# A key and value buffer of its own for the prompt's middle group, counts halved with immediates, and norm corrections with per-partition scalars

## The chip, the cores and the metric

The kernel runs on one core of a Trainium2 chip. The core's engines take their instructions in order, each from its own queue: PE (TensorE, matmuls and transposes), DVE (VectorE), ACT (ScalarE), POOL (GpSimd) and SP (SyncE, which here only issues DMAs). The metric is the time of one execution in device microseconds; several executions are made, and their median counts.

## The reference, cut to what matters

One step of a decoder layer, on a prompt of 1024 tokens and on 32 sample tokens (8 sequences of 4) with a paged cache of 8192 positions each. The layer's input is normalised, projected by one wide matrix, and goes to two groups of heads: sparse attention over the 256 best keys of each query, which an indexer chooses, and retention. What the change touches, in the reference's own lines:

```python
def _rmsnorm(x, g):
    xf = x.astype(jnp.float32)
    y = xf * lax.rsqrt(jnp.mean(xf * xf, axis=-1, keepdims=True) + EPS) * g.astype(jnp.float32)
...
    s = jnp.einsum('bqhd,bsd->bqhs', qi.astype(jnp.float32), ki.astype(jnp.float32)) * (D_IDX ** -0.5)
    score = jnp.einsum('bqh,bqhs->bqs', wi.astype(jnp.float32), jax.nn.relu(s))
    score = jnp.where(valid, score, -jnp.inf)
    top_val, top_idx = lax.top_k(score, topk)
```

The keys and values of the prompt (ka and va, 128 columns each) are also outputs.

## The kernel before

The program is written with a tile framework: the text gives a first order of the work, a scheduler turns it into one order for each engine, and pools of buffers decide which tile must wait for which transfer. A tile with the same tag in a pool takes the slots in turn; with bufs=2 the third tile waits until the first one's readers, DMAs among them, are done. The order of each engine is fixed before the program runs.

All matmuls of the projections are made from a high and a low part of x (xh, xl) and of the weights (whi, wlo), three matmuls for one product (proj_b, L257 to L259). ACT makes whi (L179), POOL makes wlo (L181). Tokens are taken in three groups, GRP: 0 to 383, 384 to 767, and 768 to 1055, the last one with the 32 sample tokens at its end.

The stages, in order of time:

- Norms of x, in nine blocks (norm_x): ACT sums squares, `rstd_of` (L233) makes 1/sqrt(v), DVE scales the block (L532), PE transposes it (L223), and ACT and DVE split it into xh and xl (L228, L229). `rstd_of` takes y, the reciprocal of a square root, and makes one correction step y·(1.5 − 0.5·v·y²) in L241 to L244. finish_y calls it nine times more near the end, ahead of the gate.
- The indexer (index_scores, L498 to L504): for each of eight blocks of queries and eight heads, PE makes the products si, ACT the relu r, DVE adds to score, and POOL puts the causal limit on the last 128 columns (affine_select, L504).
- Between these matmuls "units" of the other projections are run: four pairs of query heads (use_qa), keys and values (use_ka and use_va, weights wraw_kava), and gates (use_ga, weights wraw_ga). A staging tile with the tag qst, two buffers in the pool qsp, is shared by all of them: qst in use_qa, kst in use_ka, kvs in use_kv, sga in use_ga. Each of them ends in a DMA out of the tile.
- use_kv (L402), for each group: ACT copies the product into kvs (L406), PE transposes it into kvt (L410), DVE copies that into the second half of kvs (L412), and SP sends it out (L414). For the last group, DVE also copies the sample tokens' part (L416).
- The bisection (bisect_prompt): the 256th best score of each query is found bit by bit, in 15 steps for six blocks of queries. `count` (L651 to L665) counts the scores over a threshold cand: four blocks on DVE (L661, comparison with a sum), two on ACT as sums of signs (js, L657). ACT's sums are turned into counts by L665: cnt times −0.5 plus half the length. Then L680 and L682 choose the next cand. The first count of a bit's value, at threshold 0, runs all six blocks on DVE.
- At the same time the paged index keys of the samples are scored: POOL gathers 128 rows of 2048 (kx, L799), PE transposes them (ptx, L809), ACT copies them (kT, L810), PE multiplies (pox, L813), ACT makes a relu (rl, L816), and PE sums over heads (py, L772 and L775).
- Then retention, the samples' attention, the prompt's attention, the output projection, the norms of finish_y, and the gate.

The pool sx (L748) holds kx, kT, rl, ys, xe and the small tiles of the sample indexer. It is opened ahead of the loop over the pages and closed after it with qsp.

Of the kernel before, what the change touches and what calls it, by code (L numbers as in the profile page):

```python
# [10 lines left out]
F32 = mybir.dt.float32  # L11
# [5 lines left out]
ALU = mybir.AluOpType  # L17
# [103 lines left out]
def tile_step(ctx: ExitStack, tc: tile.TileContext, I, O):  # L121
    nc = tc.nc

    def pool(name, bufs=1, **kw):
        return tc.tile_pool(name=name, bufs=bufs, reuse_waits="tile", **kw)
# [18 lines left out]
    def bank(name, tag="b"):  # L144
        if tag in kept.get("tags", ()):
            return kept["pool"].tile([128, 512], F32, tag="s", bufs=1, name=name)
        return psum["pool"].tile([128, 512], F32, tag=tag, bufs=psum["bufs"][tag], name=name)
# [6 lines left out]
    def C(name, rows=128):  # L154
        o, w = _CW[name]
        return cst[:rows, o:o + w]
# [76 lines left out]
    def rstd_of(ss, rows, scale, name, sp):  # L233

        v = sp.tile(list(ss.shape), F32, tag="rs_v", bufs=2, name=f"rv_{name}")
        nc.vector.tensor_scalar(v[:rows], ss[:rows], scale, EPS, op0=ALU.mult, op1=ALU.add)
        y = sp.tile(list(ss.shape), F32, tag="rs_y", bufs=2, name=f"ry_{name}")
        z = sp.tile(list(ss.shape), F32, tag="rs_z", bufs=2, name=f"rz_{name}")
        nc.scalar.activation(y[:rows], v[:rows], AF.Sqrt)
        nc.vector.reciprocal(y[:rows], y[:rows])  # L240
        nc.vector.tensor_tensor(z[:rows], y[:rows], y[:rows], op=ALU.mult)  # L241
        nc.vector.tensor_tensor(z[:rows], z[:rows], v[:rows], op=ALU.mult)
        nc.vector.tensor_scalar(z[:rows], z[:rows], -0.5, 1.5, op0=ALU.mult, op1=ALU.add)
        nc.vector.tensor_tensor(y[:rows], y[:rows], z[:rows], op=ALU.mult)  # L244
        return y


# [133 lines left out]
    qsp = sxs.enter_context(pool("qsp"))  # L381
# [17 lines left out]
    v_d = dram.tile([128, 8, 128], F32, name="v_d")  # L399
    ga_d = dram.tile([128, 4, T + NS], F32, name="ga_d")  # L400

    def use_kv(g, pt, outs, outp, new):  # L402

        t0, n = GRP[g]
        st = qsp.tile([128, 2, 384], F32, tag="qst", bufs=2, name="kvs")
        nc.scalar.copy(st[:, 0, :n], pt[:, :n])  # L406
        tp = bank("kvt", "t")
        for i in range(0, n, 128):
            rows = min(128, n - i)
            nc.tensor.transpose(tp[:rows, i:i + 128], st[:, 0, i:i + rows], ident)  # L410
        nb = min(n, T - t0)
        nc.vector.tensor_copy(st[:, 1, :nb], tp[:, :nb])  # L412
        tk = st[:, 1, :nb].rearrange("p (b c) -> p b c", c=128)
        nc.sync.dma_start(outp[0, 0, t0:t0 + nb].rearrange("(b p) n d -> p b (n d)", p=128), tk)  # L414
        if g == 2:
            nc.vector.tensor_copy(new, tp[:NS, 256:384])  # L416
            nc.sync.dma_start(outs.rearrange("o b t n d -> (o b t) (n d)"), new)
        return tk
# [201 lines left out]
    NB = 6  # L620
    NA = 2
# [9 lines left out]
    def bisect_prompt():  # L631
# [5 lines left out]
        cnt = bs.tile([128, NB], F32, name="cnt")  # L637
# [7 lines left out]
        v = bs.tile([128, NB], F32, name="v")  # L645
        cf = bs.tile([128, NB], F32, name="cf")
        ge = bs.tile([128, NB], F32, name="ge")
        V = nc.vector

        def count(src, thr, op, scale=None):  # L650


            for j, o, n in lens[::-1]:
                t = thr if isinstance(thr, float) else thr[:, j:j + 1]
                if scale and j >= NB - NA:
                    js = bs.tile([128, 2 * T], BF16, tag="rk", bufs=1, name="js")
                    nc.scalar.activation(js[:, :n], src[:, o:o + n], AF.Sign, bias=t, scale=-scale,  # L657
                                         accum_out=cnt[:, j:j + 1])
                    continue
                jk = bs.tile([128, T], BF16, tag="jk", bufs=1, name="jk")  # L660
                V.tensor_scalar(jk[:, :n], src[:, o:o + n], t, None, op0=op, op1=ALU.add,  # L661
                                accum_out=cnt[:, j:j + 1])
            if scale:
                a = slice(NB - NA, NB)
                V.scalar_tensor_tensor(cnt[:, a], cnt[:, a], -0.5, C("halfn")[:, a], op0=ALU.mult, op1=ALU.add)  # L665

        for j, o, n in lens:
            V.tensor_copy(x16[:, o:o + n], s16[:, o:o + n, 1])
        yield
        count(x16, 0.0, ALU.is_ge)  # L670
        V.tensor_scalar(tb_, cnt, float(TOPK), -1.0, op0=ALU.is_lt, op1=ALU.mult)
        V.tensor_scalar(c65, cnt, float(TOPK), 65535.0, op0=ALU.is_lt, op1=ALU.mult)
# [18 lines left out]
        for j, o, n in lens:  # L691
# [3 lines left out]
                            op0=ALU.subtract, op1=ALU.mult)  # L695
            V.scalar_tensor_tensor(y16[:, o:o + n], x16[:, o:o + n], tf[:, jj], lw[:, :n],
                                   op0=ALU.is_equal, op1=ALU.mult)
# [48 lines left out]


    sx = sxs.enter_context(pool("sx", side="right"))  # L748

    wcol = sx.tile([128, 8], F32, name="wcol")  # L750
    wst = sx.tile([128, 8, 32], F32, name="wst")
# [664 lines left out]
    kvs, kws = [], []  # L1416
# [136 lines left out]
    for qb in range(8):  # L1553
# [11 lines left out]
        for kv in range(2):  # L1565
# [5 lines left out]
            for i4 in range(4):  # L1571
# [5 lines left out]
                for c in range(0, n, 512):  # L1577
# [5 lines left out]
                    for x0, x1, add in ((c, cut, mask[:, OFF.get(qb, 0) + c:OFF.get(qb, 0) + cut]),  # L1583
                                        (cut, c + wc, near[:, h - 4 * kv, cut - n + 256:c + wc - n + 256])):
                        if x1 > x0:
                            nc.vector.tensor_tensor_reduce(L[:, x0:x1], s[:, x0 - c:x1 - c], add, 1.0, least,  # L1586
                                                           op0=ALU.add, op1=ALU.min, accum_out=mn[:, i:i + 1])
# [177 lines left out]
    for cb in range(4):  # L1765
        cur, curu = wg, wu
        cs = slice(cb * 256, (cb + 1) * 256)
        for tb in (8, *range(8)):
            rows = 128 if tb < 8 else NS
# [58 lines left out]
```

## Time and profile before

| | us |
|---|---|
| median of 3 executions | 1053.49 |
| lowest and highest | 1051.36, 1053.96 |
| profiled execution | 1057.99 |
| its span | 1056.2 |
| mean granted clock of TensorE | 0.977 |

A row of the timeline has the start in us, the length in us, the engine, the line, the operation, what it writes and reads (buffer numbers left out) with the shape, and a count where equal rows in a series are put together; in brackets, how long the engine had been idle before, and who ended that. "SPq" and "POOLq" rows are DMA issues. In the list of waits a row has the engine and the tile that waited, what it waited for, the total in us, the number of times and the longest.

### The profile page before, as it was taken

How to read it: one execution, taken by the hardware profiler on the slowest of the kernel's cores; microseconds unless marked ns; L12 is line 12 of the kernel's file. 1: busy time of each engine (PE TensorE's matmuls, PEld its weight loads, DVE VectorE, ACT ScalarE, POOL GpSimd, SP SyncE). 2: the span in 40 equal slices, each digit the busy share in tenths (PEclk: the TensorE clock that was granted, in tenths of full speed). 3: DMA queues.
4: the chain of work that ended last, by engine and by line, in shares of the span. 5: the costliest groups of instructions: out<-in, count | busy, mean ns of one | idle time of the engine just before them, and what ended most of it. 6: DMA issues, size and time to landing. Idle time of an engine off the chain costs nothing.

```text
span 1056.2 us, 19867 instructions
## 1 busy us (share of the span) xinstructions
PE 994.1 (94%) x7375; PEld 836.9 (79%) x7375; DVE 678.7 (64%) x2022; ACT 504.2 (48%) x1092; POOL 322.6 (31%) x425
## 2 busy tenths in 40 slices
PE   4999998998999799998999996899999999999998
PEld 3999997766776798887888883566665899999998
DVE  6847678888492466977959937687754423773332
ACT  6546455876434377632252435556644523442211
POOL 4204123120301433525644512544330432232200
PEclk9999998998999899999999996999999999999999
DMA  8211236545353311202201724523211312432211
GB/s 294 66 60 51 95 96 208 185 130 173 123 165 108 74 42 41 61 23 87 65 22 52 180 75 136 151 76 107 79 56 42 117 41 81 136 126 87 82 38 40
DMA packets 98309, 102.24 MB, mean 97 GB/s; under 512 B 21346, under 2 KB 88386, under 8 KB 95906
## 3 DMA queue, kind: packets, MB, share of 16 engines
q1 hardware_dynamic: 92450, 74.74, 23.6%
q0 software_dynamic: 5760, 26.22, 7.9%
q8 instruction: 58, 0.95, 0.4%
q14 instruction: 41, 0.34, 0.1%
HBM read 79.25 MB, written 21.68 MB: 96 GB/s over the span
## 4 chain that ended last, share of the span: by engine, by line
PE 44%; DVE 5%; DMA 2%; POOL 2%; issue 2%; ACT 1%; SPq 0%; ACTq 0%; POOLq 0%; DVEq 0%
PE ptp L1596 4%; PE ob L1604 4%; PE pg L267 3%; PE pg L269 3%; PE pg L268 3%; PE po L267 3%; PE po L268 3%; PE po L269 3%; PE sa L1580 2%; PE sa L1581 2%; PE pvg L268 1%; PE pvg L269 1%; PE pvg L267 1%; PE pty L1651 1%; POOL wlo_vgb L181 1%
## 5 line engine op out<-in xcount | busy, mean ns | idle before, releaser
L1159 POOL DMA_INDIRECT kvs<-in_cache_kv,idx x64 | 66.7, 1042 | 78.8 <-ACT pT L1601 31.7
L267 PE MATMUL pqk<-whi_qkb,xh 128*128 128x256 f32 x256 | 75.1, 293 | 4.4 <-DVE rp L1038 4.3
L267 PE MATMUL pvg<-whi_vgb,xh 128*128 128x256 f32 x256 | 75.5, 295 | 0.5 <-ACT whi_qkb L179 0.4
L268 PE MATMUL pqk<-wlo_qkb,xh 128*128 128x256 f32 x256 | 74.3, 290 | 0.0
L268 PE MATMUL pvg<-wlo_vgb,xh 128*128 128x256 f32 x256 | 74.2, 290 | 0.0
L269 PE MATMUL pqk<-whi_qkb,xl 128*128 128x256 f32 x256 | 73.9, 289 | 0.0
L267 PE MATMUL po<-whi_o,yTh 128*128 128x256 f32 x256 | 73.2, 286 | 0.4 <-ACT yTh L1646 0.4
L269 PE MATMUL pvg<-whi_vgb,xl 128*128 128x256 f32 x256 | 73.5, 287 | 0.0
L267 PE MATMUL pg<-whi_g,yTh 128*128 128x256 f32 x256 | 72.7, 284 | 0.0
L269 PE MATMUL po<-whi_o,yTl 128*128 128x256 f32 x256 | 72.7, 285 | 0.0
L268 PE MATMUL po<-wlo_o,yTh 128*128 128x256 f32 x256 | 72.7, 284 | 0.0
L269 PE MATMUL pg<-whi_g,yTl 128*128 128x256 f32 x256 | 72.3, 283 | 0.0
L268 PE MATMUL pg<-wlo_g,yTh 128*128 128x256 f32 x256 | 72.2, 282 | 0.0
L1589 ACT ACTIVATE L<-L,mn 128x128 f32<-128x128 f32 (+7 forms) x64 | 49.6, 778 | 17.6 <-DVE mn L1586 17.0
L267 PEld LDWEIGHTS pqk<-whi_qkb,xh 128*128 128x128 f32 x256 | 49.4, 193 | 8.2 <-issue 3.5
L502 DVE SCALAR_TENSOR_TENSOR score<-r,wi,score 128x384 f32<-128x384 f32 (+5 forms) x42 | 41.0, 976 | 23.0 <-ACT r L498 21.7
L1785 DVE TENSOR_TENSOR sgm<-pu,sgm 128x256 f32<-128x256 f32 x32 | 13.6, 424 | 64.3 <-PE pu L269 60.6
L181 POOL TENSOR_TENSOR wlo_g<-wraw_g,whi_g 128x256 fp32r<-128x256 f32 x32 | 27.2, 881 | 87.4 <-ACT whi_g L179 87.3
L799 POOL DMA_INDIRECT kx<-in_cache_kidx,kidx x16 | 15.9, 995 | 116.7 <-PE ptx L809 115.8
L269 PEld LDWEIGHTS pqk<-whi_qkb,xl 128*128 128x128 f32 x256 | 49.5, 193 | 2.6 <-issue 2.4
L498 ACT ACTIVATE r<-si 128x384 f32<-128x384 f32 (+5 forms) x48 | 36.3, 758 | 32.0 <-PE si L356 30.6
L267 PEld LDWEIGHTS pvg<-whi_vgb,xh 128*128 128x128 f32 x256 | 48.5, 189 | 3.5 <-issue 0.8
(545 smaller groups left out, 3332.6 us busy)
## 6 DMA issues: line engine op xcount, KB each, us to landing
wraw_qkb<-in_w_in SPq DMA_DIRECT2D x16, 256.0 KB
wraw_vgb<-in_w_in SPq DMA_DIRECT2D x16, 256.0 KB
wraw_o<-in_w_out SPq DMA_DIRECT2D x8, 512.0 KB
qas<-qas_d SPq DMA_DIRECT2D x8, 512.0 KB
xr<-in_x_prompt SPq DMA_DIRECT2D x8, 512.0 KB
wraw_g<-in_w_ple_gate SPq DMA_DIRECT2D x8, 512.0 KB
out_y_prompt<-sgm SPq DMA_DIRECT2D x32, 128.0 KB
qas_d<-qst SPq DMA_DIRECT2D x8, 384.0 KB
```

What stands on the lines that cost most here:

```text
L181: nc.gpsimd.tensor_tensor(lo[:, a * 4 + k, :n], raw[:, k, :n], hi[:, a * 4 + k, :n].bitcast(F32), op=ALU.subtract)
L267: nc.tensor.matmul(pt[:, :n], ah, hi[:, k, :n], start=(k == 0), stop=False)
L268: nc.tensor.matmul(pt[:, :n], ah, lo[:, k, :n], start=False, stop=False)
L269: nc.tensor.matmul(pt[:, :n], al, hi[:, k, :n], start=False, stop=(k == kc - 1))
L498: nc.scalar.activation(r[:, :n], s[:, :n], AF.Relu)
L502: nc.vector.scalar_tensor_tensor(sc, r[:, :n], wi[:, qb, h:h + 1], sc, op0=ALU.mult, op1=ALU.add)
L1159: return nc.gpsimd.indirect_dma_start(out=dst, out_offset=None, in_=kvflat, in_offset=bass.IndirectOffsetOnAxis(ap=idx, axis=0))
L1580: nc.tensor.matmul(s[:, :wc], qas[:, h, :], kah[kv][:, c:c + wc], start=True, stop=False)
L1581: nc.tensor.matmul(s[:, :wc], qas[:, h, :], kal[kv][:, c:c + wc], start=False, stop=True)
L1589: behind[0] = nc.scalar.activation(L[:, :n], L[:, :n], AF.Exp, bias=least, scale=-1.0, accum_out=sm[:, i4:i4 + 1])
L1596: nc.tensor.transpose(tp[:, i4 * 128:i4 * 128 + 128], P[i4][:, kb * 128:kb * 128 + 128], ident)
L1604: nc.tensor.matmul(ob[64 * o:64 * o + 64, :256], vtok[:, kb, kv * 64:kv * 64 + 64], pT[:, o * 256:o * 256 + 256], start=(kb == 0), stop=(k ...
```

## The change

Three edits are made. In `rstd_of` the product y·y·v is one tensor_scalar with y and v as per-partition scalars, where it was two tensor_tensor; the last product is a tensor_scalar as well. In `count` the halving of ACT's sums is done with one tensor_scalar for each of the two columns, with an immediate, where it was one scalar_tensor_tensor with a constant tile. In use_kv the tile kvs of the middle group comes from a tag of its own, kvx, with one buffer in the pool sx; the other two groups stay in the shared tag.

```diff
-        nc.vector.tensor_tensor(z[:rows], y[:rows], y[:rows], op=ALU.mult)
-        nc.vector.tensor_tensor(z[:rows], z[:rows], v[:rows], op=ALU.mult)
+        nc.vector.tensor_scalar(z[:rows], y[:rows], y[:rows], v[:rows], op0=ALU.mult, op1=ALU.mult)
         nc.vector.tensor_scalar(z[:rows], z[:rows], -0.5, 1.5, op0=ALU.mult, op1=ALU.add)
-        nc.vector.tensor_tensor(y[:rows], y[:rows], z[:rows], op=ALU.mult)
+        nc.vector.tensor_scalar(y[:rows], y[:rows], z[:rows], None, op0=ALU.mult)
...
+    sxp = []
+
     def use_kv(g, pt, outs, outp, new):
...
-        st = qsp.tile([128, 2, 384], F32, tag="qst", bufs=2, name="kvs")
+        st = (sxp[0].tile([128, 2, 384], F32, tag="kvx", bufs=1, name="kvs") if g == 1 else
+              qsp.tile([128, 2, 384], F32, tag="qst", bufs=2, name="kvs"))
...
-                a = slice(NB - NA, NB)
-                V.scalar_tensor_tensor(cnt[:, a], cnt[:, a], -0.5, C("halfn")[:, a], op0=ALU.mult, op1=ALU.add)
+                for j in range(NB - NA, NB):
+                    V.tensor_scalar(cnt[:, j:j + 1], cnt[:, j:j + 1], -0.5, (j + 3) * 64.0, op0=ALU.mult, op1=ALU.add)
...
     sx = sxs.enter_context(pool("sx", side="right"))
+    sxp.append(sx)
```

Since durations and buffers are other ones, the scheduler gives other orders, also at places that the text of the change does not name. In the changed kernel the line numbers are one lower from L242 to use_kv, two higher from there to sx, and three higher behind it; L506, L663 and L802 are L504, L661 and L799 of before.

POOL at the entry of the bisection, before: kava and ga are the weights of the keys and values and of the first gates, and the last select closes the scores.

```order
L504 AFFINE_SELECT score<-score 128x128 x2
L799 DMA kx<-in_cache_kidx,kidx 128x2048 x2
L181 TENSOR_TENSOR wlo_ga_1923<-wraw_ga_1924,whi_ga_1922 128x256 x4
L181 TENSOR_TENSOR wlo_ga_1923<-wraw_ga_1931,whi_ga_1922 128x256 x4
L799 DMA kx<-in_cache_kidx,kidx 128x2048 x6
```

The same place after the change:

```order
L506 AFFINE_SELECT score<-score 128x128
L181 TENSOR_TENSOR wlo_ga_1917<-wraw_ga_1918,whi_ga_1916 128x256 x4
L506 AFFINE_SELECT score<-score 128x128
L802 DMA kx<-in_cache_kidx,kidx 128x2048 x2
L181 TENSOR_TENSOR wlo_ga_1917<-wraw_ga_1925,whi_ga_1916 128x256 x4
L802 DMA kx<-in_cache_kidx,kidx 128x2048 x6
```

Four of the eight low parts have moved ahead of the last select and of the first two gathers.

DVE at that place, before: jk with mask alone is the first count, newsc belongs to the samples' scores.

```order
L668 COPY mask<-score 128x1024
L763 TENSOR_TENSOR rn<-rn,wi 32x256
L337 SCALAR_TENSOR_TENSOR qst<-pb,qst 64x384
L661 TENSOR_SCALAR jk,cnt<-mask 128x1024
L764 TENSOR_REDUCE newsc<-rn 32x32
L661 TENSOR_SCALAR jk,cnt<-mask 128x896
L765 TENSOR_TENSOR newsc<-newsc,cst 32x32
L661 TENSOR_SCALAR jk,cnt<-mask 128x768
L766 TENSOR_TENSOR newsc<-newsc,cst 32x32
L661 TENSOR_SCALAR jk,cnt<-mask 128x640
```

After the change:

```order
L336 SCALAR_TENSOR_TENSOR qst<-pb,qst 64x256
L392 TENSOR_SCALAR qs<-pb 64x32 x2
L768 TENSOR_TENSOR newsc<-newsc,cst 32x32
L670 COPY mask<-score 128x1024
L769 TENSOR_TENSOR newsc<-newsc,cst 32x32
L427 TENSOR_TENSOR kst<-pb,kst 128x384
L759 TENSOR_TENSOR wst<-wcol,cst 128x256
L663 TENSOR_SCALAR jk,cnt<-mask 128x1024
L663 TENSOR_SCALAR jk,cnt<-mask 128x896
L663 TENSOR_SCALAR jk,cnt<-mask 128x768
```

The small work that stood between the first counts now stands ahead of them, and so do kst and wst, which stood behind the first round of the bits.

ACT at the first rounds of the bits, before: js is ACT's share of a count, kT a copy of transposed index keys.

```order
L179 CAST whi_ga_1922<-wraw_ga_1931 128x1024
L336 ACTIVATE qst<-pb 64x256 x2
L657 ACTIVATE js,cnt<-mask,cand 128x1024
L810 COPY kT<-ptx 128x1024
L657 ACTIVATE js,cnt<-mask,cand 128x896
L810 COPY kT<-ptx 128x1024
L424 CAST kst<-pb 128x384
```

After the change:

```order
L335 ACTIVATE qst<-pb 64x256
L426 CAST kst<-pb 128x384
L408 COPY kvs<-pb 128x384
L659 ACTIVATE js,cnt<-mask,cand 128x1024
L659 ACTIVATE js,cnt<-mask,cand 128x896
L813 COPY kT<-ptx 128x1024
L659 ACTIVATE js,cnt<-mask,cand 128x1024
L813 COPY kT<-ptx 128x1024
```

kst and kvs of the first group have moved ahead of the first js, and the second js has moved ahead of the first kT.

## The prediction

> **What bounds the kernel now.** I read the page's list of engines first, then busy time by stage, then what TensorE waited for, and last the rows around each place that the change touches.
>
> ```profile
> PE 994.1 (94%) x7375; PEld 836.9 (79%) x7375; DVE 678.7 (64%) x2022; ACT 504.2 (48%) x1092; POOL 322.6 (31%) x425
> ```
>
> TensorE (PE) is busy for 994.1 of 1056.2 us, and the change removes no matmul. All that it can win or lose is part of PE's 62.1 us of idle time, or of the slow clock behind an idle stretch. The columns of the next view are the stretch, its length, then the busy time of PE, PEld, DVE, ACT and POOL, and the granted clock.
>
> ```profile
> 0.00:45.00 45.00, 30.08 (x163) 26.53 (x163) 35.17 (x97) 27.80 (x58) 18.40 (x26) 1.00 0.65 211
> 105.00:168.00 63.00, 63.00 (x365) 59.49 (x365) 43.28 (x63) 33.96 (x51) 12.80 (x17) 1.00 0.29 91
> 180.00:245.00 65.00, 59.45 (x335) 41.58 (x336) 57.31 (x164) 53.33 (x90) 11.20 (x14) 0.89 0.55 181
> 245.00:330.00 85.00, 85.00 (x518) 61.77 (x517) 57.30 (x122) 39.48 (x61) 12.78 (x18) 0.99 0.42 138
> 850.00:940.00 90.00, 89.09 (x776) 85.65 (x775) 49.53 (x138) 38.75 (x108) 23.82 (x29) 1.00 0.35 108
> ```
>
> From 105 to 168 us and from 245 to 330 us PE never stands still. Time won or lost ahead of such a stretch is carried through it to the end. PE has holes in the start (14.9 us), at the entry of the bisection, and between 180 and 245 us (5.6 us, with a clock of 0.89); in the closing norms (850 to 940 us) it has 0.9 us. The waits of PE that the change can reach are these (total, times, longest):
>
> ```profile
> PE pt L223 <- DVE xl L229: 3.9, 1, 3.9
> PE pox L813 <- ACT kT L810: 2.9, 1, 2.9
> PE kvt L410 <- ACT kvs L406: 2.8, 1, 2.8
> PE pox L813 <- DVE vnew L416: 2.4, 1, 2.4
> ```
>
> **Term 1: the norms.** Each `rstd_of` loses one DVE operation, and no operation in it reads two tiles as tensors any more. Here is the chain of the third block on DVE, with the POOL group beside it.
>
> ```profile
> 12.55 0.73 DVE L241 TENSOR_TENSOR rz_x<-ry_x 128x1 f32<-128x1 f32 x1
> 13.31 0.65 DVE L242 TENSOR_TENSOR rz_x<-rz_x,rv_x 128x1 f32<-128x1 f32 x1
> 13.99 0.15 DVE L243 TENSOR_SCALAR rz_x<-rz_x 128x1 f32<-128x1 f32 x1
> 14.18 0.46 DVE L244 TENSOR_TENSOR ry_x<-ry_x,rz_x 128x1 f32<-128x1 f32 x1
> 14.68 1.72 DVE L532 SCALAR_TENSOR_TENSOR score<-score,ry_x,mask 128x1024 f32<-128x1024 f32 x1
> 13.22 6.51 POOL L181 TENSOR_TENSOR wlo_qi<-wraw_qi,whi_qi 128x256 fp32r<-128x256 f32 x8
> ```
>
> While POOL makes the low parts of a weight, an operation on one column takes 0.46 to 0.73 us when it reads tensors, and 0.15 us as L243, which has one tensor and immediates. Three operations at L243's step (13.99 to 14.18, 0.19 us) take 0.57 us in place of 2.13 us: 1.56 us less on the path to the xl for which PE waited 3.9 us. The second block's chain, free of POOL, gives one step more, 0.19. On the first block the saving is hidden:
>
> ```profile
> 7.79 1.28 DVE L532 SCALAR_TENSOR_TENSOR x<-x,ry_x,mask 128x1024 f32<-128x1024 f32 x1 [0.67 <-DMA mask<-in_g_pre]
> ```
>
> Its scaling waited 0.67 us for g_pre, and one step saved ahead of that wait is worth nothing. The bounds are 0 (another load is late next) and −1.75; I take −1.2. In the closing norms PE is 0.9 us idle in all: −0.2, between −0.9 and 0.
>
> **Term 2: the third buffer.** ACT, SP and PE at the third group of keys:
>
> ```profile
> 201.39 0.53 SPq L426 DMA_DIRECT2D ka_d<-kst  x1
> 205.44 0.39 SPq L414 DMA_DIRECT2D out_k_prompt<-kvs  x1
> 212.61 0.40 ACT L406 COPY kvs<-pb 128x288 f32<-128x288 f32 x1 [1.59 <-DMA out_k_prompt<-kvs]
> 213.06 0.81 PE L410 MATMUL kvt<-cst,kvs 128*128 128x128 f32 x3 [2.76 <-ACT kvs L406]
> 213.80 3.31 PE L813 MATMUL pox<-kT,qbd 128*64 128x512 f32 x8
> 219.00 1.08 PE L813 MATMUL pox<-kT,qbd 128*64 128x512 f32 x4
> ```
>
> The copy needs the buffer from which the second group's values go out: that transfer was issued at 205.44 and let go about 7 us later. With the second group in a tile of its own, the third group's copy waits for the transfer of the second kst, issued at 201.39 here. PE's 2.76 us go, and with them slow rows: eight pox took 3.31 us where two fours at 1.08 take 2.16. That is 2.76 + 1.15 + about 0.3 on kvt: −4.2, and −2.8 if the slow clock comes anyway.
>
> **Term 3: the counts.** Each of 15 bits gets two DVE operations for one: one step of 0.19 more, 2.9 us over 15 bits, beside PE, since DVE has 7.7 us idle from 180 to 245 us. What replaces the old form is worth more at one place:
>
> ```profile
> 234.16 3.75 DVE L665 SCALAR_TENSOR_TENSOR cnt<-cnt,cst 128x2 f32<-128x2 f32 x1 [0.82 <-ACT js L657]
> 232.32 5.56 POOL L181 TENSOR_TENSOR wlo_ga<-wraw_ga,whi_ga 128x256 fp32r<-128x256 f32 x8
> L665 DVE SCALAR_TENSOR_TENSOR cnt<-cnt,cst x15: 153/160/3745, 181.5 to 252.1; 128x2 f32<-128x2 f32 x15
> L682 DVE SCALAR_TENSOR_TENSOR cand<-gb,cand x14: 154/166/167, 181.9 to 248.0; 128x6 int32<-128x6 int32 x14
> 172.15 0.17 DVE L765 TENSOR_TENSOR newsc<-newsc,cst 32x32 f32<-32x32 f32 x1
> ```
>
> L665 ends at 237.91, when POOL's group ends (237.88); the median of the same operation is 160 ns. Queued behind it are L412 and L416, for which PE then waits 2.4 us and runs slowly after that, together about 3.3 us by the price of a cold stretch in term 2. The new operations read one tile each and an immediate, as L243 does. But L682 comes two operations later in the same round, still reads two tiles, and has met no POOL group so far (maximum 167 ns): it can be caught instead. Against that stands L765, which read two tiles in the middle of a POOL group and took 0.17 us. Half: −1.6, between −3.3 and 0.
>
> [...]
>
> **Term 4: the entry of the bisection, which the order moves.** This speaks against the change.
>
> ```profile
> 168.14 1.38 POOL L799 DMA_INDIRECT kx<-in_cache_kidx,kidx  x1 [0.57 <-issue]
> 170.80 5.58 POOL L181 TENSOR_TENSOR wlo_ga<-wraw_ga,whi_ga 128x256 fp32r<-128x256 f32 x8
> 175.11 1.94 PE L809 MATMUL ptx<-cst,kx 128*128 128x128 f32 x16 [1.09 <-DMA kx<-in_cache_kidx,kidx]
> 169.67 2.00 ACT L179 CAST whi_ga<-wraw_ga 128x1024 fp32r<-128x1024 f32 x2 [1.36 <-PE pb L258]
> 169.40:176.25 6.85, 5.32 (x12) 1.00 0.88 293
> 177.44 0.16 DVE L676 TENSOR_SCALAR cand<-tbits 128x6 int32<-128x6 int32 x1
> 177.63 1.15 ACT L657 ACTIVATE js<-mask,cand 128x1024 bf16<-128x1024 bf16 x1 [2.36 <-DVE cand L676]
> 178.90 1.01 ACT L810 COPY kT<-ptx 128x1024 f32<-128x1024 f32 x1
> 179.80 1.04 ACT L657 ACTIVATE js<-mask,cand 128x896 bf16<-128x896 bf16 x1
> 179.96 1.97 PE L813 MATMUL pox<-kT,qbd 128*64 128x512 f32 x4 [2.91 <-ACT kT L810]
> 181.21 0.42 DVE L756 TENSOR_TENSOR wst<-wcol,cst 128x256 f32<-128x256 f32 x1
> 183.19 0.56 DVE L425 TENSOR_TENSOR kst<-pb,kst 128x384 fp32r<-128x384 f32 x1
> ```
>
> (The fifth row is the busy time of L661, the counts, on DVE in that stretch.) In the order after, four of the eight wlo_ga stand ahead of the last causal select, and the two gathers behind it. The first cast ends near 170.7; four low parts take 2.8; so the select comes near 173.5 and the gather near 174.0, not 168.14. From gather to first ptx it was 6.97 us, so PE's ptx starts near 181.0 and the first half is through at 182. The mask copy waits for that select too. Behind it stand kst (0.56) and wst (0.42), and only then the six counts in one piece: mask copy and newsc until 175.8 (an estimate: select, then 2 us, of which the small work between the counts of before, 6.85 − 5.32, gives 1.5), kst and wst until 176.8, counts 5.32 until 182.1, thresholds 0.45, cand at 182.6. On ACT the second js stands ahead of the first kT: js 1.25, js 1.15, kT 1.0, and PE's pox near 186.1, not 179.96: +6.1. I take +6.0. If DVE did the same work without waiting for the select, only the moved work would count: 0.98 on DVE and the second js, 1.2: +2.2. The upper bound is +8, from ACT's copy kvs of the first group, which now stands ahead of the first js and waits for a transfer of the last query group; with the 7 us that term 2 shows for such a transfer and an issue near 175.5 it would end near 183, a js later.
>
> **Sum.** −1.2 − 0.2 − 4.2 − 1.6 + 6.0 = −1.2 us. The profiled execution took 1057.99 us, its span 1056.2, and 1.8 lie around it. It would take 1056.8. It stands 4.5 above the median of 1053.49, so beside that median I write **1052.3 us**. With all terms at their low ends: −1.75 − 0.9 − 4.2 − 3.3 + 2.2 = −8.0; at their high ends 0 + 0 − 2.8 + 0 + 8 = +5.2.
>
> **Rivals.**
>
> *The entry costs little.* DVE was filled at the entry of before, and the moved work is done earlier or later, not twice. If the last scores come early enough that DVE goes on without the hole, term 4 is +2.2 and the sum −5.0: 1048.5 us. For it: L661's 5.32 in 6.85 us show a dense DVE. Against it: four wlo_ga stand ahead of the select in POOL's queue, and the cast before them ended a wait for PE.
>
> *The bisection sets the pace (the other side).* Place: DVE and ACT from 180 to 245 us. They start 5 us later, and 11 of the rounds before 238 us are longer by 0.19 us, 2.1 together; DVE's 7.7 us idle in that stretch is then used up, and where terms 2 and 3 removed a wait, kT or kvt comes late for PE in its place. Then both gains are lost there: −1.2 − 0.2 + 6.0 = +4.6, so 1058.1 us. It decides when entry and longer rounds together pass the slack, 6.0 + 2.1 against 7.7. Against it: 3.6 us of the held L665 would be given back to DVE.
>
> *The change does not do what it says.* If the third group's copy waits for another transfer on its slot as long as before, and L682 is held, the sum is again +4.6: 1058.1. Little speaks for it: the kst transfer of the second group was issued 4 us before the values' one.
>
> **How the numbers follow.** A measurement of this kernel can tell about 0.3%, 3.2 us, from no change. The forecast's case gets 0.43, its own range is 1048 to 1056. The cheap entry gets 0.30, the paced bisection 0.22, no effect 0.05. Faster by over 3.2 us is the cheap entry nearly whole (0.28) and the low edge of the forecast (0.06): 0.34. Slower is most of the two last cases (0.23) and a high edge (0.02): 0.25. The rest, 0.41, is within. The range from 1046.5 to 1058.5 takes in the middle of each case.
>
> **What would show it.** In the profile after: no wait of kvt for kvs near 210 us, and a gather near 174 us; a first pox near 186 us; L667 never above 0.3 us, and L684 either at 0.17 or once at some us beside wlo_ga; xl of the third block 1 to 1.5 us earlier. The prediction is wrong if the first pox starts before 183 us or after 189, if a wait of PE of over 2 us appears at a place not named here, or if the stretch from 245 us on is not shifted as a whole.

## The result, and the profile after

| | before | after |
|---|---|---|
| median | 1053.49 us | 1059.92 us |
| lowest and highest of nine timed executions | 1050.99, 1056.21 | 1057.20, 1064.31 |
| profiled execution | 1057.99 us | 1057.20 us |
| its span | 1056.2 us | 1055.3 us |
| ratio, with its 95% interval | | 1.0071 [1.0050, 1.0091] |

By the ratio the change makes the kernel slower by 0.71%; the two medians differ by 6.4 us, 0.61%, which lies inside the interval. The two profiles do not show that loss as a whole: the profiled execution of before was slower than all nine timed ones of before, and the one of after is the fastest of its nine. So the profiles tell where the stages moved, and the medians tell what it came to.

First the waits of TensorE in the profile after (total, times, longest).

```profile
PE ptx L812 <- DMA kx<-in_cache_kidx,kidx: 10.3, 3, 9.2
PE pt L223 <- DVE x L534: 9.0, 1, 9.0
PE sa L1583 <- DVE mn L1589: 8.1, 1, 8.1
...
PE pt L223 <- DVE xl L229: 2.5, 1, 2.5
...
PE pb L256 <- DVE kil L349: 1.7, 1, 1.7
```

The wait of 9.2 us for the gathered keys is new. kvt's wait for kvs (2.8 before) and pox's for vnew (2.4) are gone. The wait for xl is 1.4 us shorter, and one for kil is 1.1 us longer (0.6 before). The wait for mn was 5.5 us before.

Now the stretches, with the columns of the prediction's view: PE, PEld, DVE, ACT and POOL busy, then the granted clock.

```profile
0.00:45.00 45.00, 30.47 (x171) 27.22 (x172) 32.81 (x91) 28.77 (x61) 17.85 (x26) 1.00 0.64 211
168.00:192.00 24.00, 14.06 (x78) 10.49 (x76) 22.05 (x62) 14.05 (x23) 10.35 (x13) 0.79 0.70 225
192.00:245.00 53.00, 48.98 (x307) 36.77 (x307) 46.62 (x149) 45.84 (x78) 10.29 (x13) 1.00 0.55 177
245.00:330.00 85.00, 85.00 (x527) 62.12 (x524) 57.02 (x123) 39.77 (x59) 13.40 (x17) 1.00 0.44 146
```

The same two middle stretches before:

```profile
168.00:192.00 24.00, 19.86 (x108) 13.11 (x107) 21.70 (x61) 16.87 (x27) 10.61 (x13) 0.86 0.76 263
192.00:245.00 53.00, 47.59 (x284) 35.89 (x281) 47.30 (x135) 41.88 (x72) 9.46 (x13) 0.93 0.52 167
```

From 168 to 192 us PE is busy 5.8 us less, at a clock of 0.79 instead of 0.86. From 192 to 245 us it is busy 1.4 us more, at 1.00 instead of 0.93. DVE is as full as before at the entry, while ACT has lost 2.8 us there: it waited. The entry, engine by engine, after:

```profile
169.24 3.01 POOL L181 TENSOR_TENSOR wlo_ga<-wraw_ga,whi_ga 128x256 fp32r<-128x256 f32 x4 [21.34 <-ACT whi_ga L179]
172.22 0.28 POOL L506 TENSOR_SCALAR_AFFINE_SELECT score<-score 128x128 f32<-128x128 f32 x1
172.69 1.50 POOL L802 DMA_INDIRECT kx<-in_cache_kidx,kidx  x1 [0.19 <-issue]
177.41 0.48 ACT L408 COPY kvs<-pb 128x384 f32<-128x384 f32 x1 [4.49 <-DVE jk L663]
180.99 1.15 ACT L659 ACTIVATE js<-mask,cand 128x1024 bf16<-128x1024 bf16 x1 [3.10 <-DVE cand L678]
181.57 3.65 PE L812 MATMUL ptx<-cst,kx 128*128 128x128 f32 x16 [9.21 <-DMA kx<-in_cache_kidx,kidx]
183.55 1.01 ACT L813 COPY kT<-ptx 128x1024 f32<-128x1024 f32 x1 [0.15 <-PE ptx L812]
185.15 1.11 PE L816 MATMUL pox<-kT,qbd 128*64 128x512 f32 x4
```

Two chains meet at kT. On the first, POOL does four low parts, then the select, then the gather: 172.69, 4.55 us after the gather of before (168.14). Gather to ptx takes 8.88 us where it took 6.97, and PE's 16 ptx take 3.65 us where they took 1.94: behind 9.2 us of idleness they run at a granted clock of 0.50 (181.5 to 183.5 us), where it was 1.00 before (175.1 to 177.1 us). On the second, DVE works without a hole through the mask copy, kst, wst and the six counts, so that cand is made at 180.79 and not at 177.44, and ACT makes two js ahead of kT. The first chain ends last, by 0.15 us. The first pox starts at 185.15, 5.2 us later than before (179.96).

The norm's chain of the third block in the start, on DVE, and PE behind it:

```profile
12.46 0.27 DVE L241 TENSOR_SCALAR rz_x<-ry_x,rv_x 128x1 f32<-128x1 f32 x1
12.76 0.15 DVE L242 TENSOR_SCALAR rz_x<-rz_x 128x1 f32<-128x1 f32 x1
12.95 0.21 DVE L243 TENSOR_SCALAR ry_x<-ry_x,rz_x 128x1 f32<-128x1 f32 x1
13.20 1.72 DVE L534 SCALAR_TENSOR_TENSOR score<-score,ry_x,mask 128x1024 f32<-128x1024 f32 x1
15.66 1.94 PE L223 MATMUL pt<-cst,score 128*128 128x128 f32 x8 [2.52 <-DVE xl L229]
32.48 0.44 PE L256 MATMUL pb<-xh,whi_qi 128*128 128x384 f32 x1 [1.66 <-DVE kil L349]
```

The chain lasts 0.74 us to the scaling (12.46 to 13.20) instead of 2.13 (12.55 to 14.68). Most of that comes from not being slowed beside POOL: in the second block, where POOL is idle, the chain from the start of L241 to the end of the last product takes 0.73 us before and 0.71 after. The last row is where most of the gain is given back: PE waits for kil.

And the place of the held operation:

```profile
234.47 5.58 POOL L181 TENSOR_TENSOR wlo_ga<-wraw_ga,whi_ga 128x256 fp32r<-128x256 f32 x8
235.68 0.15 DVE L667 TENSOR_SCALAR cnt<-cnt 128x1 f32<-128x1 f32 x1 [0.69 <-ACT js L659]
235.87 0.85 DVE L682 TENSOR_SCALAR gb<-cnt 128x6 int32<-128x6 f32 x1
236.75 0.66 DVE L684 SCALAR_TENSOR_TENSOR cand<-gb,cand 128x6 int32<-128x6 int32 x1
```

gb and cand take 0.85 and 0.66 us instead of 0.17 each, and DVE is through before POOL's eight low parts are (240.05). Neither is held to their end.

### The profile page after: what moved, and what is told of

It is laid out like the page before. It is cut to its first block, busy times and chain, and to the rows that moved or that the text cites. A ratio compares the mean times of both kernels' runs of the same rounds, so it can differ in the third digit from the quotient of the medians.

```text
span 1055.3 us, 19868 instructions
## 1 busy us (share of the span) xinstructions
PE 989.5 (94%) x7375; PEld 837.8 (79%) x7375; DVE 673.6 (64%) x2019; ACT 504.5 (48%) x1092; POOL 321.1 (30%) x425
## 4 chain that ended last, share of the span: by engine, by line
PE 48%; DVE 3%; DMA 2%; POOL 1%; ACT 1%; issue 1%; SPq 0%; ACTq 0%; POOLq 0%; DVEq 0%
PE ob L1607 4%; PE ptp L1599 4%; PE po L266 3%; PE pg L266 3%; PE po L268 3%; PE po L267 3%; PE pg L268 3%; PE pg L267 3%; PE sa L1583 2%; PE sa L1584 2%; PE pqk L266 1%; PE pqk L268 1%; PE pqk L267 1%; PE pvg L267 1%; PE pvg L268 1%; PE pvg L266 1%
## 5 line engine op out<-in xcount | busy, mean ns | idle before, releaser
L504 DVE SCALAR_TENSOR_TENSOR score<-r,wi,score 128x384 f32<-128x384 f32 (+5 forms) x42 | 40.9, 975 | 27.1 <-ACT r L500 26.4
L266 PEld LDWEIGHTS po<-whi_o,yTh 128*128 128x128 f32 x256 | 49.5, 193 | 2.1 <-issue 1.6
```

Of the source, the lines that this page charges most:

```text
L266: nc.tensor.matmul(pt[:, :n], ah, hi[:, k, :n], start=(k == 0), stop=False)
L504: nc.vector.scalar_tensor_tensor(sc, r[:, :n], wi[:, qb, h:h + 1], sc, op0=ALU.mult, op1=ALU.add)
```

## The experiments

Sixteen runs were made after the result, fifteen other kernels and the changed one again, each timed against before on the same chip. The median of before was 1053.49 to 1058.02 us from chip to chip, so only ratios are compared between groups. For the stages, the first starts of PE's tiles were taken from each trace: si opens the indexer, pox the samples' scores, pqk retention, sa the attention, po the output projection. The last column tells in which of three orders PE makes its matmuls from the first sa to the first po: A is the order of before (up to six matmuls apart), B that of k_buffer_only, C that of n_norms_only.

| kernel | ratio [95%] | first si | si to pox | pox to pqk | pqk to sa | sa to po | order sa to po |
|---|---|---|---|---|---|---|---|
| before | 1 | 50.4 | 129.6 | 158.1 | 304.0 | 178.8 | A |
| after | 1.0071 [1.0050, 1.0091] | 50.4 | 134.8 | 151.1 | 304.7 | 178.8 | A |
| after_again | 1.0078 [1.0057, 1.0099] | 53.2 | 134.5 | 152.1 | 305.4 | 182.5 | A |
| n_norms_only | 1.0071 [1.0042, 1.0100] | 50.3 | 135.0 | 156.2 | 306.5 | 176.1 | C |
| c_counts_only | 0.9987 [0.9963, 1.0011] | 50.1 | 129.5 | 155.1 | 305.7 | 179.0 | A |
| k_buffer_only | 1.0008 [0.9988, 1.0029] | 51.0 | 129.4 | 158.5 | 307.6 | 177.6 | B |
| ck_counts_and_buffer | 0.9997 [0.9977, 1.0017] | 51.1 | 129.4 | 156.1 | 308.4 | 177.5 | B |
| a_entry_restored | 1.0007 [0.9991, 1.0022] | 50.4 | 129.5 | 156.4 | 305.7 | 173.8 | C |
| a_train_with_gaps | 1.0097 [1.0068, 1.0127] | 50.3 | 134.8 | 156.3 | 305.3 | 178.5 | A |
| b_train_with_gaps | 1.0009 [0.9988, 1.0030] | 50.6 | 129.4 | 156.1 | 306.0 | 174.3 | A |
| ck_train_with_gaps | 0.9998 [0.9981, 1.0014] | 50.8 | 129.4 | 155.4 | 305.7 | 174.5 | B |
| b_low_on_dve | 0.9974 [0.9954, 0.9994] | 50.8 | 129.5 | 152.8 | 306.4 | 174.5 | B |
| k_low_on_dve | 0.9988 [0.9972, 1.0005] | 50.7 | 129.5 | 149.5 | 306.2 | 181.2 | A |
| ck_low_on_dve | 0.9965 [0.9946, 0.9984] | 51.0 | 129.5 | 149.4 | 304.4 | 182.9 | A |
| a_restored_low_on_dve | 0.9944 [0.9922, 0.9967] | 51.1 | 129.6 | 149.9 | 303.3 | 177.5 | B |
| a_low_on_dve | 1.0051 [1.0032, 1.0070] | 52.0 | 134.1 | 151.4 | 305.7 | 182.5 | A |
| a_restored_low_state_late | 0.9946 [0.9924, 0.9969] | 50.9 | 129.5 | 151.6 | 305.1 | 179.3 | A |
| k_state_late | 1.0015 [0.9993, 1.0038] | 50.7 | 129.5 | 155.2 | 304.3 | 180.3 | A |

One column sorts the ratios: the five rows with 134 to 135 us from si to pox are the five that are slower by over 0.3%. From the first po to the end it is 234.5 to 237.9 us, and no longer in these five (234.5 to 236.6).

The last column matters too. In order A the stage from sa to po took 178.5 to 183.0 us in ten of eleven profiles and 174.3 in one; in orders B and C it took 173.8 to 177.6 in all seven. So two kernels whose letters differ also differ in this stage, by some 4 us in the profiles, whatever else was changed in them. What the order is worth in the medians was not measured.

### The parts of the change alone

The norms alone, the counts alone, the buffer alone, and the two last together, each put into the kernel before:

```diff
 # n_norms_only: rstd_of as in the change, nothing else
+        nc.vector.tensor_scalar(z[:rows], y[:rows], y[:rows], v[:rows], op0=ALU.mult, op1=ALU.mult)
...
+        nc.vector.tensor_scalar(y[:rows], y[:rows], z[:rows], None, op0=ALU.mult)
 # c_counts_only: count as in the change, nothing else
+                    V.tensor_scalar(cnt[:, j:j + 1], cnt[:, j:j + 1], -0.5, (j + 3) * 64.0, op0=ALU.mult, op1=ALU.add)
 # k_buffer_only: kvs of the middle group in its own tag, nothing else
+        st = (sxp[0].tile([128, 2, 384], F32, tag="kvx", bufs=1, name="kvs") if g == 1 else
 # ck_counts_and_buffer: the two together, the norms as before
```

> Only the norms' edit; counts and buffers as before. Its order has the entry of the change on POOL, DVE and ACT (low parts ahead of the last select, counts behind kst and wst, two js ahead of the first kT). Theory 'entry': start -1.3, entry +6, the wait of kvt for kvs and the held L665 stay: +4.5 us (about 1058). Rival 'pace' (the bisection's longer rounds eat the gains of buffer and counts): it needs the entry too, so +4.5 as well. Rival 'executions differ, not kernels': 0.

> Only the halving by immediates; the order on POOL, ACT, PE and SP is that of before. Theory 'entry': between 0 (L682 is held in place of L665) and -3.3 us (no hold, no wait of PE for vnew). Rival 'pace': rounds are longer by 0.19 us, so 0 to +2.

> Only the third buffer; the entry of the bisection is that of before. Theory 'entry': the wait of kvt for kvs goes, -4 us (about 1049.5). Rival 'pace': the wait comes back as one for DVE or ACT, 0 to -1.

> Counts and buffer without the norms' edit; the entry is that of before. Theory 'entry': the change without its loss, -4 to -7 us (1046.5 to 1049.5). Rival 'pace': 0.

The norms alone bring the whole loss, 1.0071 (7.5 us, between 4.4 and 10.6, where 4.5 was expected), and their order of the entry is that of the whole change. In n_norms_only PE's rows at the entry are these:

```profile
181.76 3.65 PE L808 MATMUL ptx<-cst,kx 128*128 128x128 f32 x16 [9.42 <-DMA kx<-in_cache_kidx,kidx]
185.34 1.19 PE L812 MATMUL pox<-kT,qbd 128*64 128x512 f32 x4
```

The three kernels without the norms' edit keep the entry of before (pox 129.4 to 129.5 us behind si), and none of them differs measurably from before. The buffer alone is worth +0.8 us (−1.3 to +3.1), which excludes the expected −4; both together −0.3 us (−2.4 to +1.8), which excludes −4 to −7; the counts −1.4 us (−3.9 to +1.2), which excludes neither nothing nor the forecast. So the edits on which the prediction counted for gains gave none that can be measured. The traces show one reason. (The profiles of k_buffer_only and ck_counts_and_buffer are the slowest of the twelve executions of each, so they need not tell what a median execution does.) In k_buffer_only kvt no longer waits for kvs, but DVE has this, beside POOL's gather and low parts:

```profile
230.25 0.94 POOL L803 DMA_INDIRECT kx<-in_cache_kidx,kidx  x1 [17.50 <-PE ptx L813]
230.70 6.10 DVE L683 TENSOR_SCALAR gb<-cnt 128x6 int32<-128x6 f32 x1
231.21 5.56 POOL L181 TENSOR_TENSOR wlo_ga<-wraw_ga,whi_ga 128x256 fp32r<-128x256 f32 x8
```

The operation that makes gb ends at 236.80, when POOL's series ends (236.77). It is held for 6.1 us where L665 was held for 3.75, and PE waits 3.7 us for it:

```profile
PE pox L817 <- DVE gb L683: 3.7, 1, 3.7
```

From pox to pqk the kernel needs 158.5 us, before 158.1: in this execution the gain is exchanged for a longer hold. n_norms_only holds the same operation for 6.10 us, ck_counts_and_buffer the one that makes cand, for 5.90. In c_counts_only gb meets the series 1.39 us behind its start, as in after, and takes 0.85 us; that stage is 3.0 us shorter.

### The entry restored

The last product of the norm is a tensor_tensor again, all else as in the change; with that, the scheduler puts out POOL's entry of before.

```diff
-        nc.vector.tensor_scalar(y[:rows], y[:rows], z[:rows], None, op0=ALU.mult)
+        nc.vector.tensor_tensor(y[:rows], y[:rows], z[:rows], op=ALU.mult)
```

> The whole change, except that the last product of the norm's correction is a tensor_tensor again. With that the order has the entry of before: both selects and both gathers ahead of the eight wlo_ga, the first counts spread ahead of kst and wst, js and kT in turn. Theory 'entry': the gather is issued near 168 us, the first ptx starts near 175, and the 7.5 us that the change lost are gone: 0 +- 2 us against before. Rival 'the forms themselves' (the scalar forms take longer than the tensor forms, in all three places): only one operation of nine calls is taken back, so +6 to +7.5 stays.

```profile
168.14 1.35 POOL L802 DMA_INDIRECT kx<-in_cache_kidx,kidx  x1 [0.60 <-issue]
175.20 1.94 PE L812 MATMUL ptx<-cst,kx 128*128 128x128 f32 x16 [1.22 <-DMA kx<-in_cache_kidx,kidx]
179.88 1.97 PE L816 MATMUL pox<-kT,qbd 128*64 128x512 f32 x4 [2.74 <-ACT kT L813]
```

The gather, ptx and pox stand where they stood before, and the loss is gone: 1.0007, as the theory had it (0 ± 2 us). This form of one product changes the order in other stages too, the attention's among them. But n_norms_only and a_entry_restored have the same order on PE, DVE, ACT and POOL from the first sa to the first po, and differ by 0.64% as well; of the 6.5 us between their profiles, 5.5 lie between si and pox. Their orders also differ in the start, in the bisection and behind the first po, but there a_entry_restored wins nothing (first si 50.4 against 50.3 us, pox to pqk 156.4 against 156.2, po to the end 236.9 against 235.1). So the late entry is the cause, and not the attention's order. No gain remains, though the buffer is in: the hold is there, 5.90 us (on cand), and PE then waits 3.6 us for DVE.

### Gaps in POOL's series

Does the hold last for the series because its eight operations stand end to end? In three kernels (the change, before, counts with buffer) a memset of one column was put behind each low part of these gates, and each next one tied behind it:

```diff
+                if name == 'ga1':
+                    with tc.issue_after(li.ins):
+                        gap[0] = nc.gpsimd.memset(gap_, 0.0).ins
```

> The whole change, and a one-column memset on POOL behind each of the eight low parts of the second gate weights; the order on all other engines is that of the change. Theory 'entry': the loss is made at the entry, so +5 to +7.5 us against before stay, less what a held operation costs in some executions (0 to -3). Rival 'the hold is the loss': near 0. If a memset doesn't let DVE in between, a held operation of over 3 us is still to be seen.

> The kernel before with the same eight memsets; the order on all other engines is that of before. It measures the hold alone: if L665 (or L680, L682) is held for 4 to 6 us in most executions, -3.3 us; if only in a few, 0 to -1. The wait of kvt for kvs stays.

> Counts and buffer without the norms' edit, and the eight memsets; the order on all other engines is that of ck_counts_and_buffer, which measured 0. Theory 'hold takes the place of the buffer wait': without a hold the buffer's 4 us come out, -4 to -6 us against before (and no held operation in its profile). Rival 'the time is given back later' (retention and attention have waits that take up any earlier start): 0 +- 1.5 again.

The ratios are those of the kernels without memsets, or worse. The hold is there in all three profiles: 4.45 us on gb in a_train_with_gaps, 4.57 on the halving (L665 of before) in b_train_with_gaps, and 6.13 on cand in ck_train_with_gaps. So these runs do not say what a kernel without the hold would take, and decide none of the expectations about that. In a_train_with_gaps, which at +0.97% is slower than was expected:

```profile
236.83 0.73 POOL L184 TENSOR_TENSOR wlo_ga<-wraw_ga,whi_ga 128x256 fp32r<-128x256 f32 x1
237.50 4.45 DVE L689 TENSOR_SCALAR gb<-cnt 128x6 int32<-128x6 f32 x1
237.56 0.73 POOL L184 TENSOR_TENSOR wlo_ga<-wraw_ga,whi_ga 128x256 fp32r<-128x256 f32 x1
...
241.16 0.72 POOL L184 TENSOR_TENSOR wlo_ga<-wraw_ga,whi_ga 128x256 fp32r<-128x256 f32 x1
```

gb starts 0.06 us ahead of the third low part and ends at 241.95, 0.07 us behind the eighth. The memsets in between did not let it through. In after gb began at 235.87, at the boundary of the second and the third part (two of 5.58 / 8, 1.40 us behind 234.47), and was through after one more. What decides at such a boundary was not found.

### The low parts on DVE

The eight low parts of these gates are made by DVE, so POOL has no series beside the bisection. DVE takes 0.42 us for each; in b_low_on_dve the eight take 2.8 us one behind the other.

```diff
-                nc.gpsimd.tensor_tensor(lo[:, a * 4 + k, :n], raw[:, k, :n],
+                (nc.vector if name == 'ga1' else nc.gpsimd).tensor_tensor(lo[:, a * 4 + k, :n], raw[:, k, :n],
```

It was put into before, the buffer alone, counts with buffer, the change with the entry restored, and the change itself.

> The kernel before, with the eight low parts of the second gate weights made on DVE and not on POOL (about 3 us of DVE work in the bisection): no POOL train is left there that could hold a small operation. The wait of kvt for kvs stays (2.5 to 2.9 us). Theory 'the hold takes the gain': -1 to -3 us against before. Rival 'given back later': 0 +- 1.

> The third buffer alone, again with those low parts on DVE. Theory 'the hold takes the gain' (with the buffer the order puts a small operation of DVE right where POOL's train begins, and it is held for 6.1 us): now the buffer's gain comes out, 3 to 5 us less than b_low_on_dve. Rival 'given back later': equal to b_low_on_dve within 1 us, although the wait of kvt is gone.

> Counts and buffer with those low parts on DVE, no norms' edit. Theory 'the hold takes the gain': as k_low_on_dve, within 1.5 us, since the counts' form matters only through the hold. Rival 'given back later': equal to before.

> a_entry_restored with those low parts on DVE: the whole change but for one form, with the entry of before and no train in the bisection. Theory 'entry and hold': all three gains, 1.2 + 4 + some of the hold's: -4 to -7 us against before, the fastest of all. Rival 'given back later': 0 +- 1.5.

> The changed kernel, its late entry kept, with the eight low parts ga1 on DVE, so that nothing can be held beside them. It differs from a_restored_low_on_dve (0.9944) in the entry alone. Theory (the late entry costs PE 5 to 6 us whatever follows): 0.999 to 1.001; first ptx near 181, pox near 185. Rival (the late entry costs time only because it puts the rounds of the bisection and POOL's low parts together; without a hold the bisection makes the delay good): 0.994 to 0.996, as with the entry restored.

The changed kernel itself was run once more beside it, as it is (after_again).

> The changed kernel once more, so that it stands beside the next run on the same chip. Theory (the entry costs some 6 us, and a hold of a small DVE operation by POOL's eight low parts comes in most executions): 1.006 to 1.009 of before; in the profile the first ptx near 181.5, pox near 185, and, unlike in the first profile, an operation of 3.7 to 6.1 us beside the eight low parts. Rival (the first profile, which had no hold, is the rule for this kernel): the same time, and again no operation on DVE that is held beside the low parts.

Before gains 0.26% [0.06, 0.46], 2.7 us, as expected. How much of that is the hold is not shown: the work moved too, PE's wait of kvt for kvs was 1.1 us in b_low_on_dve and not the expected 2.5 to 2.9, and the attention's order changed from A to B. With the series gone, pox to pqk takes 152.8 us, with the buffer as well 149.5: in the profiles, 3.3 us of the buffer's gain come out there. But k_low_on_dve should have been 3 to 5 us faster than b_low_on_dve, and is not: 0.9988 against 0.9974. Its attention has order A again, and from sa to po it takes 6.7 us longer (181.2 against 174.5). So what the buffer is worth without the series stays open. ck_low_on_dve came out 2.4 us below k_low_on_dve, where 1.5 was allowed; their intervals overlap. With the entry restored and the low parts on DVE, the change gives the fastest kernel found, 0.9944, 5.9 us under before.

PE's entry in a_low_on_dve, which differs from that kernel in the text by the form of one product:

```profile
182.56 3.65 PE L812 MATMUL ptx<-cst,kx 128*128 128x128 f32 x16 [8.54 <-DMA kx<-in_cache_kidx,kidx]
186.13 1.48 PE L816 MATMUL pox<-kT,qbd 128*64 128x512 f32 x4
```

and in a_restored_low_on_dve:

```profile
175.89 1.94 PE L812 MATMUL ptx<-cst,kx 128*128 128x128 f32 x16 [1.17 <-DMA kx<-in_cache_kidx,kidx]
180.66 1.77 PE L816 MATMUL pox<-kT,qbd 128*64 128x512 f32 x4 [2.84 <-ACT kT L813]
```

The rival, that without a hold the bisection makes the late entry good, falls: 1.0051 against 0.9944. But the theory's number was missed as well, 0.999 to 1.001. The two kernels differ by 1.07%, 11 us, more than twice what their traces show up to pox (4.5 us, 134.1 against 129.6). But they do not differ in the entry alone, as had been assumed: the attention's order is A in the one and B in the other, and from sa to po it is 182.5 against 177.5 us. So the 11 us are not the price of the entry.

after_again was expected to show a hold, and shows none: gb took 0.85 us, as in the first profile. That part of the theory fell: the hold belongs to neither profile of after. Its ratio repeats the first.

### The state update at the end of retention

In the traces with the buffer, and in n_norms_only without it, PE's wait for the attention's first mn is 7.9 to 8.1 us, before 5.5. In k_buffer_only and a_restored_low_on_dve DVE's order differs there: the update of the samples' state (sso), which waits for PE's dst, stands ahead of the norm's gz. These two kernels got it back behind gz:

```diff
+        while late:
+            with tc.issue_after(gz_[0]):
+                late.pop()()
```

> The entry restored, the low parts on DVE, and in retention's last pair of heads the state update of the samples (sso) put behind the norm's gz, as it stands in the kernel before. Theory (the change's order put sso, which waits for PE's dst, ahead of gz; that is 2.6 us of PE's wait for the attention's first mn): that wait 5.5 instead of 8.1 us, and 0.991 to 0.993 of before, 2 to 3 us less than at 0.9944. Rival (the longer wait is made up by the stage behind it, where DVE and ACT set the pace): the wait is 5.5 us and the time stays at 0.994 to 0.995.

> The buffer alone, with sso behind gz in the same way; the low parts stay on POOL, so the held operation stays. k_buffer_only was 1.0008. Theory (of the 4.2 us that the third buffer should bring, a longer hold takes 2 to 3 and sso 2.6): 0.997 to 0.999, the wait for mn 5.5, a held operation of about 6 us still there. Rival (sso's place costs nothing in the end): 1.000 to 1.001.

The wait became shorter in both, as in k_state_late (longest 4.8 us; 8.1 in k_buffer_only):

```profile
PE sa L1596 <- DVE mn L1602: 7.5, 3, 4.8
```

The times did not: 0.9946 where it was 0.9944, and 1.0015 where it was 1.0008. The stage from sa to po took 1.8 and 2.7 us longer. The rival gave the right times. But the edit also changed the attention's order from B to A in both kernels, and A is the longer one in the profiles. So it is not shown whether the place of sso costs something: its gain may have been paid back by that order.

## Why the prediction was wrong, step by step

**Term 4, the entry (+6.0).** Right in mechanism and nearly in size. The gather came at 172.69 (expected near 174.0), pox at 185.15 (near 186.1; the bound was 183 to 189). kT stood behind two js and PE's ptx, as worked out. Gather to ptx took 8.88 us, not the 6.97 that the step took over from before, while the select came 1.3 us earlier than estimated; these two partly cancel. cand came at 180.8, not 182.6. ACT's kvs, the upper bound's mishap, was done at 177.89 and held nothing. The rival of the cheap entry (+2.2) is excluded.

**Term 1, the start (−1.2).** xl came 1.5 us earlier, as forecast, and it was worth nothing at the end of the stage: the first si starts at 50.4 us in both. Most of it went at kil (0.6 to 1.7 us), a wait that the prediction had not followed. It had named 0 as the bound "another load is late next"; it was a later DVE operation. The step of 0.19 us for each new operation was too small: the two products with per-partition scalars took 0.27 and 0.21 us, so the chain of the third block lasts 0.74 us and not 0.57, and a block free of POOL gains next to nothing (0.73 to 0.71 us) where one step of 0.19 was counted.

**Terms 2 and 3 (−4.2 and −1.6).** In the two profiles of after both are as forecast: no wait for kvs, no hold, L667 at most 0.155 us. Pox to pqk took 151.1 and 152.1 us instead of 158.1: −7.0 and −6.0, where the two terms said −5.8, in one execution each. cand (L682 before, L684 after), of which the prediction said that it could be caught instead, was not held in after; in ck_counts_and_buffer and a_entry_restored it was, for 5.90 us. In ck_train_with_gaps it was held for 6.13. In n_norms_only, k_buffer_only, k_state_late and a_train_with_gaps gb was held, which the prediction had not named at all. What it set against a hold, L765 with two tiles in 0.17 us beside POOL's group, was one-sided: L766, an operation of the same form and size, took 0.54 us there (173.13, before).

The prediction had set the new forms apart by what they read: one tile and an immediate, as L243, where L665 and L682 read two tiles. The number of tiles alone does not sort the runs. gb has one input and six columns and was held for 6.10 us (k_buffer_only); the halving (L667 in after), one input and one column, ran beside the low parts once in each of after, after_again, c_counts_only and a_train_with_gaps and took 0.15 to 0.16 us. Whether the columns, the place in the series or something else decides between these two was not shown.

**The sum, and the step that failed.** For the profiled execution it was 1056.8 us, and after's first profile took 1057.20. What failed is the size of terms 2 and 3, and with it the step "It stands 4.5 above the median of 1053.49, so beside that median I write 1052.3 us". That step supposes that the median execution of before has the same waits to lose as the profiled one, and that after's median stands as far below its profile. Neither held. The profiled execution of before was longer than all nine timed ones, and after's median stands 2.7 above its profile. The runs say what the terms are worth in the timed executions. The third buffer is worth +0.8 us (−1.3 to +3.1) and not −4.2, nor the −2.8 that was its high end; buffer and counts together are worth −0.3 us (−2.4 to +1.8) and not −5.8. Without these 5.8 us the prediction's own sum is +4.6, 1058.1 us. The rest is term 1, which gave nothing, and the entry, whose price in the ratios is 0.64% or 6.7 us, where 6.0 was forecast. That price is from n_norms_only and a_entry_restored, which share the attention's order; the intervals of the two leave 3 to 10 us. With buffer and counts at about 0 and the norms' edit, which brings the late entry, at the 0.71% that it costs alone, the 0.71% of the whole change is there.

Why the buffer's gain does not appear is only in part shown. In the five profiles with the buffer, the old entry and POOL's series, a hold of 5.9 to 6.1 us takes its place and PE waits 3.6 to 3.8 us. In the two profiles of after there is no such hold, and the ratio is no better than that of the norms alone.

One wait that no term had grew as well: PE's wait for mn, from 5.5 to 8.1 us. The stage from sa to po, which it opens, was as long as before (178.8 us).

**The rival of the paced bisection** gave 1058.1, near the result, by a mechanism that the profiles do not show: from pox on, the bisection of after was shorter, not longer. PE's small waits in it (rl, xe, ys, kT, each at most 0.8 us) are far from eating both terms. The third rival gave 1058.1 too. Its first condition did not occur, since kvt no longer waits for kvs; its second, a hold of the operation that makes cand, occurred in a_entry_restored, ck_counts_and_buffer and ck_train_with_gaps, but not in after.

**What stays open.** Up to pox the late entry shows 4.5 to 5.5 us in every trace. The 6.7 us of the ratios are not more than their interval allows. How long a stage takes differs from execution to execution as well. In after_again the start is 2.8 us longer, behind a slow clock in it,

```profile
30.00:40.00 10.00, 8.35 (x44) 7.88 (x42) 7.02 (x21) 6.24 (x17) 3.41 (x5) 0.83 0.54 158
```

and sa to po 3.7 us longer than before. But a_entry_restored had a clock of 0.83 in the same stretch and no later si, and sa to po took 174.3 and 182.9 us in two kernels with the same order on PE (b_train_with_gaps and ck_low_on_dve). One execution each can't sort that. Open too are the mean time of the holds in executions without a profile, and what the attention's orders are worth in the medians.

## What to carry to other kernels

Another form of a small operation can change a scheduler's order far away; price the new order, and if it starts a long load later, look for a form that keeps the old order. Before a difference between two kernels is put down to an edit, compare their orders in all stages: here three comparisons were spoilt by another order of the attention. Before counting a wait as gain, ask whether the profiled execution is a typical one: if it is longer than the timed ones, its waits may be what makes it so. Where another engine's series can hold a small operation, moving one operation out of its way can just change which one is held (L665 for 3.75 us in before, gb for 6.10 us in k_buffer_only); here taking the series away gained 0.26% in the kernel before and 0.63% in the change with its old entry (1.0007 to 0.9944), with other things moved in both.

## What the hardware showed that was not expected

- An operation with one input, 128x6 from float to integer, was held for 6.10 us beside POOL, longer than the operation with two inputs in the kernel before (3.75): both ended with the series, and it began earlier. It was held from within POOL's gather (230.70, the gather from 230.25 to 231.19) to the end of the eight low parts behind it. The same operation beside a gather without low parts behind it took 0.17 us (before, 187.63).
- The hold of gb did not end between two of POOL's eight low parts (6.10 us in k_buffer_only), not even with a memset between them (4.45 us over six of the eight, in a_train_with_gaps). But an operation that began at the boundary of two parts got through after one (0.85 us, in after, after_again and c_counts_only).
- From issue of the gather to the first transpose it took 6.97 us before and 8.88 after, for the same transfer. The DMA engines were busy for 0.73 of the time in between before and for 0.91 after; that this is the reason was not tested.
- On one column, a product with two per-partition scalars took 0.25 to 0.28 us in all 18 places of after, with one 0.19 to 0.22, with immediates 0.14 to 0.16, beside work of POOL or not. The tensor forms of before took 0.13 to 0.16 us in most places and up to 1.03 us in some.
